# Modulation's PSUM bank, the y loads and the final projection put in another order, with the opening's modulation first

## The chip, the cores and the metric

The kernel runs on one core of one Trainium2 chip. The metric is the device time of one execution in microseconds (us), taken as the median of several runs. TensorE (PE) multiplies, with its weight loads shown apart (PEld); VectorE (DVE), ScalarE (ACT) and GpSimd (POOL) do elementwise work; SyncE (SP) issues every transfer here, on one queue.

## The reference

Two layers over 256 context tokens and 1024 latent tokens with 1024 features, then a last norm of the latent tokens. Every layer has the same frame:

```python
def rmsnorm(x, w):
    xf = x.astype(F32)
    y = xf * lax.rsqrt(jnp.mean(xf * xf, axis=-1, keepdims=True) + RMS_EPS)
    return (y * w.astype(F32)).astype(x.dtype)

def modulate(h, shift, scale):
    return h * (1 + scale) + shift
```

Shift, scale and gate of a layer come from one small product: SiLU of the conditioning vector (another one for context tokens) times a 1024 x 3072 matrix, plus a bias. Layer 0 projects the modulated input to two branches. Branch A is a bidirectional linear recurrence (RG-LRU) behind a short convolution, with sigmoid gates; branch B is attention in a band of 128 tokens to each side plus the context. Each is multiplied by its own SiLU gate, and the concatenation goes through one output projection. Layer 1 is a bidirectional gated linear recurrence in chunks (HGRN2) with eight heads, again with an output projection. Each projection is multiplied by the gate and added to the stream.

## The kernel before

Everything is held feature-major: 128 features on the partitions, tokens along the free dimension. The tokens form three chunks: c=0 and c=1 are 512 latent tokens each, c=2 is the 256 context tokens. A float32 product is made from three matmuls over split values (high and low part of the weight, high and low part of the data: `mm3`, `steps3`, line 104). `load_w` fetches a weight (line 90), ScalarE makes w_hi (line 94), GpSimd, or with `split` GpSimd and VectorE by halves, makes w_lo (line 95).

TensorE's order is that of the code in three stretches (`order_0` for the opening, `order_pe` for attention, `order_c` for layer 1 and the end). Each other engine has one fixed order too, which the scheduler chose from dependences and priorities when the program was built; `tc.high_priority` moves an instruction ahead of others that could stand there. Tiles come from pools with a number of buffers for each tag; who asks for a buffer waits until its last reader is done.

The places of this case:
- **Opening.** `load_x(c)` fetches xin of a chunk. `rms0(c)` squares its eight feature blocks on ScalarE, adds them in pairs on VectorE (line 283), sums over the partitions by matmuls n_ps with a column of ones (line 287), and spreads the reciprocal root n_r over the partitions by transposes n_pr (line 229) and a copy to n_rs (line 231). `ada_mm(l, g)` multiplies four loaded `ada` tiles by the conditioning vectors (ps_m, line 164; 32 matmuls) and copies the result to adar; `ada_fin` transposes it (ps_c, line 175), adds the bias to get mods (line 177) and, for scales, amul. `first(g, c)` applies norm and modulation to feature blocks 2g and 2g+1 of a chunk (`norm_mod`: xin, u_hi, u_lo, lines 249 to 251), then runs the first two weights' matmuls on them.
- **The loop over j = 0..7** of branch A: projection to X (line 399 copies it), convolution, gates (12 blocks of matmuls into three PSUM banks "gate"; line 437 and its neighbour apply sigmoids), two scans, products into sga. At the end of each turn one `ada_mm` runs, and its `ada_fin` runs in the next turn after X's matmuls. ps_m and ps_c share one PSUM bank, "ada".
- **out_B.** The attention output, in DRAM as yb_d, is fetched as yr and split into y_hi and y_lo (`load_yB`), and projected in a loop over eight output blocks m. acc (what branch A left, hA_d in DRAM) is loaded by line 775; VectorE adds to it (line 781).
- **The end.** `out_early` projects seven of the eight heads for chunk 0 while the last head is worked on. Then a loop over m adds the eighth head for chunk 0 (`out_m(0, full, ...)`) and makes the first half of chunk 1; a second loop makes the second half of chunk 1. Line 1051 evacuates PSUM into h; `sumsq` squares it (ScalarE, line 193) and adds into n_ss (VectorE, line 194). `final_norm` makes n_rs from n_ss (lines 212 to 231) and multiplies all eight blocks by it (line 1111).

Of the kernel before, what the change touches and what calls it, by code (L numbers as in the profile page):

```python
# [50 lines left out]
def backbone_kernel(ctx: ExitStack, tc: tile.TileContext, a: dict, out):  # L51
# [82 lines left out]
    def drain(*gens):  # L134
        for g in gens:
            for _ in g:
                pass
# [32 lines left out]
    def ada_mod(wpool, psp, l, g, bufs=NADA):  # L170
        ada_fin(psp, ada_mm(wpool, psp, l, g, bufs), l, g)

    def ada_fin(psp, row, l, g):
        pc = psp.tile([128, 512], F32, tag="ada", name="ps_c", bufs=1)
        PE.transpose(pc[:, :128], row, ident)
        with tc.high_priority(offset=PRI_E):
            V.tensor_tensor(out=mods[:, l, g], in0=pc[:, :128].rearrange("p (b x) -> p b x", x=32)[:, :, 0:2],
                            in1=adab[:, l, g].unsqueeze(2).to_broadcast([128, 4, 2]), op=ALU.add)
            if g < 4:
                V.scalar_tensor_tensor(out=amul[:, l, 2 * g:2 * g + 2], in0=mods[:, l, g, 2:4], scalar=1.0,  # L180
                                       in1=normw[:, l * 8 + 2 * g:l * 8 + 2 * g + 2].unsqueeze(2)
                                       .to_broadcast([128, 2, 2]), op0=ALU.add, op1=ALU.mult)
# [34 lines left out]
    def mean_rs(np_, ps, n):  # L217

        nb = n // 128
        r1 = np_.tile([128, 4], F32, tag="n_r1", name="n_r1", bufs=2)  # L220
        S.activation(r1[:, :nb], ps[:, :nb], AF.Sqrt, bias=eps_c)  # L221
        V.reciprocal(r1[:, :nb], r1[:, :nb])  # L222
        return r1

    def spread_rs(np_, psp, r1, n, tag, bufs, rtag="n_rs"):
        nb = n // 128
        pr = psp.tile([128, 4, 128], F32, tag=tag, name="n_pr", bufs=bufs)
        for b in range(nb):
            PE.transpose(pr[:, b], r1[:, b:b + 1].to_broadcast([128, 128]), ident)  # L229
        rs = np_.tile([128, n], F32, tag=rtag, name="n_rs", bufs=1, padded_shape=[128, 512])  # L230
        S.copy(rs, pr[:, :nb].rearrange("p a b -> p (a b)"))  # L231
        return rs

    def new_u(up, c):
        return tuple(up.tile([128, 8, CHUNKS[c][1]], F32R, tag=f"u_{p}{c}", name=f"u_{p}{c}") for p in ("hi", "lo"))
# [38 lines left out]
    def rms0(c):  # L274

        n = CHUNKS[c][1]
        ps = psA.tile([128, 512], F32, tag="gate", name="n_ps", bufs=3)
        sums = []
        for k in range(0, 8, 2):
            sq = [p0.tile([128, n], F32, tag="n_sq", name="n_sq", bufs=SQB, padded_shape=[128, 512]) for _ in range(2)]  # L280
            for i in range(2):
                S.activation(sq[i], xin[c][:, k + i], AF.Square)
            V.tensor_tensor(out=sq[0], in0=sq[0], in1=sq[1], op=ALU.add)
            sums.append(sq[0])
        for b in range(n // 128):
            for i in range(4):
                PE.matmul(ps[:, b:b + 1], sums[i][:, b * 128:b * 128 + 128], ones_m[:, 0:1], start=(i == 0),
                          stop=(i == 3))
        rs0[c] = spread_rs(p0, psA, mean_rs(p0, ps, n), n, "gate", 3, f"n_rs{c}")

    rs0 = {}

# [10 lines left out]
    def gemm_steps(w, c, psp, tag, bufs):  # L303
# [2 lines left out]
        yield from steps3(ps[:, :n], gemm_terms(w, c), n)  # L306
        return ps[:, :n]

    u = [new_u(up, c) for c in range(3)]
    apool, apool_st = open_pool("apool", side="right")  # L310

    order_0 = tc.manual_schedule(engines={PE.engine})
    order_0.__enter__()
    load_x(2)
    load_x(0)
    rms0(2)
    rms0(0)
    ada_mod(apool, psA, 0, 0, 8)
    w_first = [load_w(a["w0"][i], split=True) for i in (0, 8)]
    ps_first = {}  # L320

    def first(g, c):
# [6 lines left out]
        for i in range(2):  # L329
            mm3(ps_first[i, c], [(w_first[i][0][:, k * 128:k * 128 + 128], w_first[i][1][:, k * 128:k * 128 + 128],  # L330
                                  u[c][0][:, k], u[c][1][:, k]) for k in (2 * g, 2 * g + 1)], g == 0, g == 3)

    first(0, 2)
    row = ada_mm(apool, psA, 0, 1, 8)
    load_x(1)
    first(0, 0)
    ada_fin(psA, row, 0, 1)
    first(1, 2)
    first(1, 0)
    rms0(1)  # L340
# [62 lines left out]
    for j in range(8):  # L403
# [20 lines left out]
        if j < 7:  # L424
            X_next = x_proj(j + 1)
        if j:
            ada_fin(psA, row, *ada_lg)
        R, I, A, M = ([rg.tile([128, W], F32, tag=t_, name=t_, bufs=2) for _ in range(2)] for t_ in "RIAM")

        for d in range(2):  # L430
# [338 lines left out]
    hp0, hp0_st = open_pool("hp0")  # L769
    acc, n1ss = {}, {}  # L770

    def out_B(cs, yB, npool, psp, tag, bufs):
        for c in cs:
            acc[c] = npool.tile([128, 8, CHUNKS[c][1]], F32, tag=f"acc{c}", name=f"acc{c}")
            SY.dma_start(acc[c], hA_d[c])
            n1ss[c] = npool.tile([128, CHUNKS[c][1]], F32, tag=f"n1ss{c}", name="n1ss")
        for m in range(8):
            w = load_w(a["wo0"][8 + m], split=cs == (1,))
            for c in cs:
                ps, gt = out_half(w, m, yB[c], c, psp, tag, bufs)  # L780
                V.scalar_tensor_tensor(out=acc[c][:, m], in0=ps, scalar=gt, in1=acc[c][:, m],  # L781
                                       op0=ALU.mult, op1=ALU.add)
                if c < 2:
                    SY.dma_start(h1_d[:, m, c * 512:c * 512 + 512], acc[c][:, m])
                sumsq(npool, n1ss[c], acc[c][:, m], m)

    def load_yB(c):
        yB[c] = new_y(c)
        for k in range(8):
            split_y(yrp, yb_d[k // 2][c][:, k % 2], CHUNKS[c][1], *yB[c], k)  # L790

    yB = {}
    load_yB(2)
    load_yB(0)
    load_yB(1)
    out_B((2, 0), yB, hp0, psB, "mmo", 2)
    psB_st.close()
    psC, psC_st = open_pool("psC", space=PSUM)
    hp, hp_st = open_pool("hp", side="right")
# [245 lines left out]
    def out_m(c, sl, m, ks, w, ss=None):  # L1045

        n = sl.stop - sl.start
        ps = psC.tile([128, 512], F32, tag="mm", name="mm_o", bufs=4)
        yield from steps3(ps[:, :n], [(w[0][:, i * 128:i * 128 + 128], w[1][:, i * 128:i * 128 + 128],
                                       yT[c][:, k, 0, sl], yT[c][:, k, 1, sl]) for i, k in ks], n)  # L1050
        V.scalar_tensor_tensor(out=h2[c][:, m, sl], in0=ps[:, :n], scalar=mods[:, 1, 4 + m // 4, m % 4, 0:1],  # L1051
                               in1=h2[c][:, m, sl], op0=ALU.mult, op1=ALU.add)
        if ss is not None:
            sumsq(fq, ss, h2[c][:, m, sl], m if sl.start == 0 else (m - 4) % 8)

    full = slice(0, 512)

# [66 lines left out]
    for m in range(8):  # L1124
        w = ws[m] = load_m(m) if m > 1 else last_w[1 + m]
        SY.dma_start(h2[1][:, m], h1_d[:, m, 512:1024])
        drain(out_m(0, full, m, [(m, 7)], wk, ss[0]))
        drain(out_m(1, half[0], m, [(k, k) for k in range(8)], w, ss[1]))
    norms = [final_norm(0, full, ss[0]), final_norm(1, half[0], ss[1])]
    for g in norms:  # L1130
        next(g)
    for m in (4, 5, 6, 7, 0, 1, 2, 3):
        if m in (6, 7):
            drain(norms.pop(0))

        drain(out_m(1, half[1], m, [(k, k) for k in range(8)], ws[m] if m > 3 else load_m(m), ss[2]))
# [90 lines left out]
```

## Time and profile before

| | us |
|---|---|
| median of three runs | 1970.53 (1968.96 to 1972.46) |
| the profiled execution | 1970.83 |
| its span | 1969.0 |
| TensorE busy in it | 1877.2 (95%) |
| VectorE busy | 1134.1 (58%) |
| ScalarE busy | 954.6 (48%) |
| GpSimd busy | 467.0 (24%) |

The span goes from the first to the last instruction in the trace; 1.8 us of the execution's time lie around it. Shares are of the span. The granted clock of TensorE was 0.986 on the mean; it has two levels, 1.0 (2.4 GHz) and 0.5 (1.2 GHz).

### The profile page before, as it was taken

The numbers are of one execution on the slowest core, as the hardware profiler recorded it, in microseconds if no ns is written. First come the engines' busy times: TensorE is split into PE (matmuls) and PEld (weight loads), VectorE is DVE, ScalarE is ACT, GpSimd is POOL, SyncE is SP. The second block draws the span as 40 slices with busy tenths as digits, with TensorE's granted clock in tenths as the row PEclk, the third lists the DMA queues.
The fourth block names the chain that finished last, engine by engine and source line by source line (L and its number), as shares of the span: only waits on it lengthen the run. The fifth ranks groups of instructions, "written<-read, shape, count | busy, mean of one in ns | idle before, by whom it ended". The sixth has DMA issues, their size and how long they took to land. (4 is left out here: it accounts for less than half of the span.)

```text
span 1969.0 us, 36589 instructions
## 1 busy us (share of the span) xinstructions
PE 1877.2 (95%) x15228; PEld 1599.7 (81%) x15228; DVE 1134.1 (58%) x1920; ACT 954.6 (48%) x1766; POOL 467.0 (24%) x309
## 2 busy tenths in 40 slices
PE   6989999999999999999998999999999999999896
PEld 5778888889888787788777889888887987888686
DVE  3766555554456555656534757375557447555656
ACT  4478666683146668555642442443443334334332
POOL 0133323330111114213232212121221122122342
PEclk8999999999999999999999999999999999999998
DMA  8222333322633436435435231111111101011643
GB/s 320 88 97 92 110 102 107 99 100 101 198 113 103 128 101 192 144 119 174 142 115 201 92 109 45 33 55 35 45 52 34 53 29 61 23 54 39 252 142 115
DMA packets 89462, 207.53 MB, mean 105 GB/s; under 512 B 9808, under 2 KB 38224, under 8 KB 88272
## 3 DMA queue, kind: packets, MB, share of 16 engines
q1 hardware_dynamic: 89296, 205.20, 31.6%
q8 instruction: 119, 1.95, 0.4%
q14 instruction: 47, 0.39, 0.1%
HBM read 155.36 MB, written 49.81 MB: 104 GB/s over the span
## 5 line engine op out<-in xcount | busy, mean ns | idle before, releaser
L95 POOL TENSOR_TENSOR w_lo<-w_raw,w_hi 128x1024 fp32r<-128x1024 f32 (+2 forms) x137 | 314.9, 2302 | 1109.3 <-ACT w_hi L94 1059.7
L104 PE MATMUL mm<-u_hi,w_hi 128*128 128x512 f32 (+1 forms) x1456 | 547.3, 376 | 6.7 <-DVE sga L423 3.7
L104 PE MATMUL mm<-u_lo,w_hi 128*128 128x512 f32 (+1 forms) x1456 | 527.6, 362 | 4.9 <-DVE u_lo L251 4.9
L104 PE MATMUL mm<-u_hi,w_lo 128*128 128x512 f32 (+1 forms) x1456 | 527.3, 362 | 0.0
L104 PEld LDWEIGHTS mm<-u_hi,w_hi 128*128 128x128 f32 x1456 | 276.1, 190 | 54.5 <-issue 9.3
L104 PEld LDWEIGHTS mm<-u_lo,w_hi 128*128 128x128 f32 x1456 | 276.8, 190 | 42.4 <-DVE u_lo L251 6.9
L104 PEld LDWEIGHTS mm<-u_hi,w_lo 128*128 128x128 f32 x1456 | 275.9, 189 | 43.2
L94 ACT CAST w_hi<-w_raw 128x1024 fp32r<-128x1024 f32 (+2 forms) x163 | 141.7, 884 | 195.3 <-PE mm L104 77.8
L104 PE MATMUL mmo<-y_hi,w_hi 128*128 128x512 f32 (+1 forms) x384 | 146.1, 380 | 7.4 <-DVE acc L781 7.4
L600 DVE CUSTOM_DVE_ANT_0 p<-s_ps,maskA 128x640 f32<-128x640 f32 (+2 forms) x160 | 110.4, 713 | 59.6 <-PE s_ps L595 59.5
L611 ACT ACTIVATE p<-p,nm 128x640 f32<-128x640 f32 (+2 forms) x160 | 118.7, 743 | 42.8 <-DVE nm L607 39.2
L104 PE MATMUL mmo<-y_hi,w_lo 128*128 128x512 f32 (+1 forms) x384 | 137.5, 358 | 0.0
L104 PE MATMUL mmo<-y_lo,w_hi 128*128 128x512 f32 (+1 forms) x384 | 137.0, 357 | 0.0
L628 ACT COPY pt<-t 128x512 f32<-128x512 f32 x168 | 94.7, 581 | 82.5 <-PE t L625 82.1
L104 PE MATMUL mm_v<-w_hi,u_hi 128*128 128x256 f32 x400 | 115.2, 288 | 0.0
L104 PE MATMUL mm_v<-w_lo,u_hi 128*128 128x256 f32 x400 | 113.1, 283 | 0.0
L104 PE MATMUL mm_v<-w_hi,u_lo 128*128 128x256 f32 x400 | 113.1, 283 | 0.0
L946 DVE TENSOR_TENSOR KK<-KK,tot 128x1280 f32<-128x1280 f32 x48 | 80.1, 1670 | 41.0 <-PE lv L932 23.9
L625 PE MATMUL t<-ident,p 128*128 128x128 f32 x672 | 98.5, 274 | 4.3 <-ACT pt L628 2.7
L104 PE MATMUL mm_o<-yT,w_hi 128*128 128x256 f32 (+1 forms) x384 | 92.1, 334 | 8.2 <-DMA yT<-y_d 3.1
L625 PEld LDWEIGHTS t<-ident,p 128*128 128x128 f32 x672 | 80.7, 141 | 19.1 <-ACT pt L628 4.7
L104 PEld LDWEIGHTS mmo<-y_hi,w_hi 128*128 128x128 f32 x384 | 73.4, 191 | 22.4 <-issue 8.1
(219 smaller groups left out, 3462.6 us busy)
## 6 DMA issues: line engine op xcount, KB each, us to landing
w_raw<-w_in SPq DMA_DIRECT2D x66, 512.0 KB, 3.7
ada<-ada_w_in SPq DMA_DIRECT2D x48, 512.0 KB, 6.4
w_raw<-wo_in SPq DMA_DIRECT2D x32, 512.0 KB, 3.7
qt<-q_d SPq DMA_DIRECT2D x20, 512.0 KB, 4.9
y_d<-yhl SPq DMA_DIRECT2D x14, 512.0 KB, 3.1
yT<-y_d SPq DMA_DIRECT2D x14, 512.0 KB, 11.0
w_raw<-wo1m_in SPq DMA_DIRECT2D x12, 512.0 KB, 3.8
xin<-hT_in SPq DMA_DIRECT2D x5, 1024.0 KB, 9.2
```

The source lines that it names most:

```text
L94: S.copy(hi[:, o:m], raw[:, o:m])
L95: eng.tensor_tensor(out=lo[:, o:m], in0=raw[:, o:m], in1=hi[:, o:m].bitcast(F32), op=ALU.subtract)
L104: ins = PE.matmul(ps, l, r, start=(first and i == 0), stop=(last and i == n - 1))
L600: V.tensor_tensor_reduce(out=p[:, :nk], in0=s_ps[:, c0[x]:c0[x] + nk], in1=self.msks[x], scale=1.0, scalar=NEG, op0=ALU.add, op1=ALU.max, ...
L611: S.activation(p, p, AF.Exp, scale=0.125, bias=nm[:, x:x + 1], accum_out=dn[:, x:x + 1])
L625: PE.transpose(pt[:, h], self.P[h][:, o:o + 128], ident)
L628: S.copy(ptc, pt)
L946: V.tensor_tensor(out=kv_, in0=kv_, in1=custom(tot, 1, [[2, nb // 2], [nb - 1, 2], [0, hb]]), op=ALU.mult)
```

## The change

It has four parts.
- The opening: modulation's first product stands ahead of the two large chunks. The transfers are asked for as xin of chunk 2, ada, the first two weights, xin of chunk 0, ada, xin of chunk 1. `rms0` adds the squares in fours instead of pairs, so half as many n_ps matmuls are left. `warm(n)` issues n matmuls of a constant by itself into a PSUM tile that nothing reads.
- In the loop over j, `ada_fin` copies ps_c to SBUF on ScalarE, and VectorE reads the copy.
- In out_B, the fetching and splitting of chunk 1's y goes, one block at a time, between the weights of the first loop.
- At the end, half 0 of chunk 1 goes ahead of chunk 0's last term, the final norms begin behind the second loop's first block, and evacuation and `sumsq` in `out_m` have a high priority.

```diff
-    def ada_fin(psp, row, l, g):
+    def ada_fin(psp, row, l, g, pool=None):
         pc = psp.tile([128, 512], F32, tag="ada", name="ps_c", bufs=1)
         PE.transpose(pc[:, :128], row, ident)
         with tc.high_priority(offset=PRI_E):
-            V.tensor_tensor(out=mods[:, l, g], in0=pc[:, :128].rearrange("p (b x) -> p b x", x=32)[:, :, 0:2],
+            mc = pc[:, :128].rearrange("p (b x) -> p b x", x=32)[:, :, 0:2]
+            if pool:
+                m_sb = pool.tile([128, 4, 2], F32, tag="m_sb", name="m_sb", bufs=2)
+                S.copy(m_sb, mc)
+                mc = m_sb
+            V.tensor_tensor(out=mods[:, l, g], in0=mc,
...
             V.tensor_tensor(out=sq[0], in0=sq[0], in1=sq[1], op=ALU.add)
+            if k % 4:
+                V.tensor_tensor(out=sq[0], in0=sq[0], in1=sums.pop(), op=ALU.add)
             sums.append(sq[0])
         for b in range(n // 128):
-            for i in range(4):
+            for i in range(2):
...
-        rs0[c] = spread_rs(p0, psA, mean_rs(p0, ps, n), n, "gate", 3, f"n_rs{c}")
+        r1 = mean_rs(p0, ps, n)
+        warm(4)
+        rs0[c] = spread_rs(p0, psA, r1, n, "gate", 3, f"n_rs{c}")
...
+    def warm(n):
+
+        ps = psA.tile([128, 512], F32, tag="gate", name="ps_w", bufs=3)
+        for _ in range(n):
+            PE.matmul(ps[:, :128], ones_m, ones_m, start=True, stop=True)
...
     load_x(2)
-    load_x(0)
+    warm(20)
     rms0(2)
-    rms0(0)
-    ada_mod(apool, psA, 0, 0, 8)
+    row = ada_mm(apool, psA, 0, 0, 8)
+    warm(3)
+    ada_fin(psA, row, 0, 0)
     w_first = [load_w(a["w0"][i], split=True) for i in (0, 8)]
...
+    load_x(0)
+    warm(16)
     first(0, 2)
+    rms0(0)
+    warm(8)
+    first(0, 0)
     row = ada_mm(apool, psA, 0, 1, 8)
     load_x(1)
-    first(0, 0)
+    warm(3)
     ada_fin(psA, row, 0, 1)
+    warm(8)
     first(1, 2)
     first(1, 0)
     rms0(1)
...
-            ada_fin(psA, row, *ada_lg)
+            ada_fin(psA, row, *ada_lg, rg)
...
             w = load_w(a["wo0"][8 + m], split=cs == (1,))
+            if beside:
+                next(beside)
...
             split_y(yrp, yb_d[k // 2][c][:, k % 2], CHUNKS[c][1], *yB[c], k)
+            yield
...
-    load_yB(2)
-    load_yB(0)
-    load_yB(1)
-    out_B((2, 0), yB, hp0, psB, "mmo", 2)
+    drain(load_yB(2), load_yB(0))
+    out_B((2, 0), yB, hp0, psB, "mmo", 2, load_yB(1))
...
+        drain(out_m(1, half[0], m, [(k, k) for k in range(8)], w, ss[1]))
         drain(out_m(0, full, m, [(m, 7)], wk, ss[0]))
-        drain(out_m(1, half[0], m, [(k, k) for k in range(8)], w, ss[1]))
     norms = [final_norm(0, full, ss[0]), final_norm(1, half[0], ss[1])]
-    for g in norms:
-        next(g)
-    for m in (4, 5, 6, 7, 0, 1, 2, 3):
-        if m in (6, 7):
+    for i, m in enumerate((4, 5, 6, 7, 0, 1, 2, 3)):
+        if i == 1:
+            for g in norms:
+                next(g)
+        if i in (2, 3):
             drain(norms.pop(0))
```

TensorE's order at the very start of the program, before (mm is first's product, w_hi and w_lo its weight):

```order
L287 MATMUL n_ps<-ones_m,n_sq 128x1 x8
L229 MATMUL n_pr<-ident,n_r_176 128x128 x2
L287 MATMUL n_ps<-ones_m,n_sq 128x1 x16
L229 MATMUL n_pr<-ident,n_r_221 128x128 x4
L164 MATMUL ps_m<-ada,cc 32x128 x32
L175 MATMUL ps_c<-ident,adar 128x128
L104 MATMUL mm<-u_hi_137,w_hi 128x256
```

The same place in the changed program:

```order
L322 MATMUL ps_w<-ones_m 128x128 x20
L294 MATMUL n_ps<-ones_m,n_sq 128x1 x4
L322 MATMUL ps_w<-ones_m 128x128 x4
L234 MATMUL n_pr<-ident,n_r_193 128x128 x2
L164 MATMUL ps_m<-ada,cc 32x128 x32
L322 MATMUL ps_w<-ones_m 128x128 x3
L175 MATMUL ps_c<-ident,adar 128x128
L322 MATMUL ps_w<-ones_m 128x128 x16
L104 MATMUL mm<-u_hi_137,w_hi 128x256
```

Chunk 0's norm (16 n_ps and 4 n_pr) has gone from ahead of ps_m to behind first's products of chunk 2.

SyncE's queue ahead of out_B, before (yb_d is the attention output by head group, hA_d_80 what branch A left for chunk 2, hA_d_78 for chunk 0):

```order
L90 DMA w_raw<-wo_in 128x1024
L692 DMA yr<-yb_d_70 128x512
L692 DMA yr<-yb_d_73 128x512 x2
L775 DMA acc_9922<-hA_d_80 128x2048
L692 DMA yr<-yb_d_76 128x512 x2
L775 DMA acc_9925<-hA_d_78 128x4096
```

The same stretch of the changed program:

```order
L90 DMA w_raw<-wo_in 128x1024
L797 DMA acc_9967<-hA_d_80 128x2048
L797 DMA acc_9970<-hA_d_78 128x4096
L714 DMA yr<-yb_d_70 128x512
L714 DMA yr<-yb_d_73 128x512
L90 DMA w_raw<-wo_in 128x1024
L808 DMA h_d<-acc_9970 128x512
```

Both loads of acc have moved ahead of the last five yr loads, which now stand among the loop's weights and stores.

VectorE in the second loop of the end, before (h_17743 is chunk 0, h_18387 chunk 1):

```order
L1051 SCALAR_TENSOR_TENSOR h_18387<-mm_o,mods,h_18387 128x256 x2
L194 TENSOR_TENSOR n_ss<-n_ss,n_sq 128x256
L1111 SCALAR_TENSOR_TENSOR h_17743<-h_17743,fnw,n_rs 128x512 x8
L1051 SCALAR_TENSOR_TENSOR h_18387<-mm_o,mods,h_18387 128x256 x2
L1111 SCALAR_TENSOR_TENSOR h_18387<-h_18387,fnw,n_rs 128x256
L194 TENSOR_TENSOR n_ss<-n_ss,n_sq 128x256
L1111 SCALAR_TENSOR_TENSOR h_18387<-h_18387,fnw,n_rs 128x256 x7
```

The same place in the changed program (h_17822 is chunk 0, h_18466 chunk 1):

```order
L1135 SCALAR_TENSOR_TENSOR h_17822<-h_17822,fnw,n_rs 128x512 x3
L1075 SCALAR_TENSOR_TENSOR h_18466<-mm_o,mods,h_18466 128x256
L1135 SCALAR_TENSOR_TENSOR h_17822<-h_17822,fnw,n_rs 128x512
L199 TENSOR_TENSOR n_ss<-n_ss,n_sq 128x256
L1135 SCALAR_TENSOR_TENSOR h_17822<-h_17822,fnw,n_rs 128x512 x3
L1075 SCALAR_TENSOR_TENSOR h_18466<-mm_o,mods,h_18466 128x256
L1135 SCALAR_TENSOR_TENSOR h_17822<-h_17822,fnw,n_rs 128x512
L199 TENSOR_TENSOR n_ss<-n_ss,n_sq 128x256
L1135 SCALAR_TENSOR_TENSOR h_18466<-h_18466,fnw,n_rs 128x256 x2
```

The eight products of the final norm, one block before, are now cut by evacuations and sums.

## Rows read from the trace of the kernel before

**Rows 1.** The page: span, and TensorE's busy time with its share.
```profile
span 1969.0 us, 36589 instructions
PE 1877.2 (95%) x15228; PEld 1599.7 (81%) x15228; DVE 1134.1 (58%) x1920; ACT 954.6 (48%) x1766; POOL 467.0 (24%) x309
```
**Rows 2.** Waits of TensorE over the span: total us, times, longest us.
```profile
PE n_ps L287 <- DVE n_sq L283: 11.1, 5, 8.5
PE mmo L104 <- DVE acc L781: 7.4, 2, 6.8
PE n_ps L212 <- DVE n_ss L194: 5.3, 3, 2.9
PE ps_m L164 <- DVE mods L177: 5.0, 1, 5.0
...
PE mm_o L104 <- ACT n_rs L231: 2.0, 1, 2.0
...
PE mm_o L104 <- POOL w_lo L95: 1.7, 2, 1.1
```
**Rows 3.** Windows: stretch, its length, busy us by engine, PEclk, DMA share, GB/s.
```profile
8.00:30.00 22.00, 16.85 (x119) 14.80 (x119) 5.15 (x12) 9.81 (x22) 0.00 (x0) 1.00 1.01 406
57.00:81.00 24.00, 22.73 (x208) 18.07 (x198) 22.35 (x42) 12.56 (x22) 2.58 (x1) 0.96 0.23 65
141.00:148.00 7.00, 6.29 (x38) 4.54 (x40) 0.65 (x2) 3.57 (x5) 1.08 (x1) 0.51 0.55 187
1035.00:1043.00 8.00, 3.75 (x20) 3.75 (x21) 2.53 (x4) 3.03 (x5) 4.91 (x3) 0.57 0.90 315
1892.00:1899.00 7.00, 5.82 (x25) 5.62 (x26) 2.48 (x3) 0.63 (x1) 0.58 (x1) 0.51 0.00 0
1929.00:1934.00 5.00, 4.66 (x26) 4.69 (x27) 0.36 (x2) 0.26 (x1) 0.00 (x0) 0.66 0.01 3
1933.00:1961.00 28.00, 22.94 (x190) 22.50 (x189) 20.93 (x31) 8.24 (x15) 9.97 (x4) 0.99 0.38 132
```
**Rows 4.** Timeline of the opening: start us, busy us, engine, idle before.
```profile
7.28 1.95 ACT L282 ACTIVATE n_sq<-xin 128x256 f32<-128x256 f32 x6 [3.61 <-DMA xin<-hT_in]
...
24.53 1.12 PE L229 MATMUL n_pr<-ident,n_r 128*128 128x128 f32 x4 [0.57 <-DVE n_r L222]
...
37.65 2.39 PE L164 MATMUL ps_m<-ada,cc 128*32 128x128 f32 x64
...
51.18 3.63 PE L287 MATMUL n_ps<-ones_m,n_sq 128*128 128x1 f32 x32
...
56.27 0.58 ACT L231 COPY n_rs<-n_pr 128x512 f32<-128x512 f32 x1 [1.17 <-PE n_pr L229]
56.89 1.41 DVE L249 SCALAR_TENSOR_TENSOR xin<-xin,amul,n_rs 128x512 f32<-128x512 f32 x2 [1.57 <-ACT n_rs L231]
```
**Rows 5.** Timeline of turn j=1 at the gates.
```profile
135.63 0.58 ACT L399 COPY X<-mm 128x512 f32<-128x512 f32 x1
...
141.71 0.63 PE L164 MATMUL ps_m<-ada,cc 128*32 128x128 f32 x2 [5.04 <-DVE mods L177]
```
**Rows 6.** Timelines of SyncE's queue, VectorE and TensorE at out_B's start.
```profile
1030.81 0.42 SPq L775 DMA_DIRECT2D acc<-hA_d  x1
...
1038.71 0.48 DVE L781 SCALAR_TENSOR_TENSOR acc<-mmo,mods,acc 128x256 f32<-128x256 f32 x1 [1.23 <-DMA acc<-hA_d]
...
1039.25 0.58 PE L104 MATMUL mmo<-y_hi,w_hi 128*128 128x256 f32 x1 [6.83 <-DVE acc L781]
```
**Rows 7.** Timelines of TensorE and VectorE in the end's two loops.
```profile
1893.18 0.79 PE L104 MATMUL mm_o<-yT,w_hi 128*128 128x512 f32 x1 [1.97 <-DVE yT L1036]
...
1938.61 2.41 DVE L194 TENSOR_TENSOR n_ss<-n_ss,n_sq 128x256 f32<-128x256 f32 x1 [0.84 <-ACT n_sq L193]
1940.94 9.73 DVE L1111 SCALAR_TENSOR_TENSOR h<-h,fnw,n_rs 128x512 f32<-128x512 f32 x8
...
1959.49 0.42 DVE L194 TENSOR_TENSOR n_ss<-n_ss,n_sq 128x256 f32<-128x256 f32 x1 [0.54 <-ACT n_sq L193]
```

More of the change, by code (lines that the diff above doesn't have):

```diff
@@ L283, in rms0 @@
             V.tensor_tensor(out=sq[0], in0=sq[0], in1=sq[1], op=ALU.add)
+            if k % 4:
+                V.tensor_tensor(out=sq[0], in0=sq[0], in1=sums.pop(), op=ALU.add)
             sums.append(sq[0])
         for b in range(n // 128):
-            for i in range(4):
+            for i in range(2):
                 PE.matmul(ps[:, b:b + 1], sums[i][:, b * 128:b * 128 + 128], ones_m[:, 0:1], start=(i == 0),
-                          stop=(i == 3))
-        rs0[c] = spread_rs(p0, psA, mean_rs(p0, ps, n), n, "gate", 3, f"n_rs{c}")
+                          stop=(i == 1))
+        r1 = mean_rs(p0, ps, n)
+        warm(4)
+        rs0[c] = spread_rs(p0, psA, r1, n, "gate", 3, f"n_rs{c}")
     rs0 = {}
@@ L770, in backbone_kernel, with out_B @@
     acc, n1ss = {}, {}
-    def out_B(cs, yB, npool, psp, tag, bufs):
+    def out_B(cs, yB, npool, psp, tag, bufs, beside=None):
         for c in cs:
@@ L1050, in out_m @@
                                        yT[c][:, k, 0, sl], yT[c][:, k, 1, sl]) for i, k in ks], n)
[L1051 to L1054, printed above, removed]
+        with tc.high_priority(offset=PRI_E):
+            V.scalar_tensor_tensor(out=h2[c][:, m, sl], in0=ps[:, :n], scalar=mods[:, 1, 4 + m // 4, m % 4, 0:1],
+                                   in1=h2[c][:, m, sl], op0=ALU.mult, op1=ALU.add)
+            if ss is not None:
+                sumsq(fq, ss, h2[c][:, m, sl], m if sl.start == 0 else (m - 4) % 8)
     full = slice(0, 512)
```

## The prediction

> **What bounds the kernel now.** The first view is the page's count of busy time: TensorE works 1877.2 of 1969.0 us [rows 1], so what the change can win is what TensorE idles, about 90 us, and what it loses at the lower clock. The second is the table of TensorE's waits: squares of the first norms 11.1 us, acc 7.4, sums of the last norms 5.3, mods 5.0, n_rs 2.0, w_lo 1.7 [rows 2]. These six stand in the four places that the change touches; they sum to 32.5 us. The third is the table of windows: right behind a long wait the granted clock is 0.51 to 0.66 [rows 3], which is mostly the lower of the two levels (1.2 for 2.4 GHz), so a wait costs more than its length: a matmul in such a stretch takes about twice as long. The last view is the timeline around each wait, to see who is late and what is late next.
>
> The profiled execution took 1970.83 us, 1.8 more than its span and 0.3 more than the median; the sum is made against it.
>
> **Part A, the opening.** Before, xin2 is there at 7.28, when ScalarE begins its squares [rows 4], and everything up to 30 us moves at 406 GB/s [rows 3], so the order of the queue decides what can start. Behind xin2 now stand four ada tiles and two weights (3.1 MB) and then xin0 (2.1 MB): 5.2 MB at 406 GB/s is 12.9 us, so xin0 is complete at 20.1. TensorE does modulation and chunk 2 meanwhile. Squares of xin0, at 0.6 us each (twice the 0.33 of a 256-column one, [rows 4]) and with ScalarE also busy with chunk 2's u_hi, end between 23 and 25.3. Behind them, step by step: the sums in fours 1.4; 8 matmuls n_ps 1.8 (32 records took 3.63 [rows 4], each matmul makes two); 4 constant products and 4 transposes 1.9 (x4 took 1.12 [rows 4]); the copy 0.6 [rows 4]; two products, u_hi and u_lo 2.2 (0.70 for a product [rows 4]); 12 matmuls 2.8. first(0,0) thus ends at about 34.6. The rest up to chunk 1's norm (ps_m, ps_c, mods, first(1,2), first(1,0)) lay before between ps_m's start at 37.65 and n_ps's at 51.18 [rows 4], 13.5 with first(0,0)'s 2.8 among them, so 10.7 now: to 45.3. From there to the copy of n_rs were 5.1 (51.18 to 56.27, [rows 4]); half the n_ps records save 1.8, 4 constant products add 0.8: 4.1. n_rs of chunk 1 would be copied at 49.4 if the clock holds, against 56.27; where one or two of the waits lower the clock again, each costs 1 to 1.5, so I take 51.0. From there on, VectorE and TensorE have the same work in the same order: VectorE is busy 22.35 of 24 us between 57 and 81 [rows 3], so what is won ahead of it shifts it as a whole. **Gain 5.3 us** (3 to 7.5). The 70 constant products are nothing on the sum where they stand in waits: at 0.15 to 0.28 each (1.12 for four [rows 4]) they are 10 to 20 us, and the waits that they stand in are the 11.1 for squares [rows 2] and those for mods and u_hi behind them. Without that cover, the 16 ahead of first(0,2) could last up to 2 us longer than the wait for u, which is in the lower bound. Four extra adds on VectorE (0.7 each) stand in the sums' 1.4.
>
> **Part B, the bank.** In turn j=1 TensorE reached the next ps_m at 136.67 and waited 5.04 us for mods [rows 5], which stands on VectorE behind scans and products; both use the one bank "ada". Behind the wait the clock is 0.51 over 6.29 us of work [rows 3]; at full clock these would take 3.2, so 3.1 are lost at most, and I take 2.8, since matmuls this short do not halve in full. Now ScalarE copies ps_c right behind X's last copy, which ends at 136.21 [rows 5]; an 128x8 copy I put at 0.2 (nothing so small is in the rows; the 128x512 one is 0.58 [rows 5], the upper bound), so the bank is free at about 136.4, before TensorE asks. **Gain 5.04 + 2.8 - 0.2 = 7.6** (5 to 8.3). The other six turns show no such wait (the table has one, [rows 2]), so they win nothing. What they pay is one copy on ScalarE, ahead of the gates' sigmoids; with three banks for gates, 0.2 per turn hides behind the matmuls of the next gate. mods itself stays late on VectorE, and nothing reads it until layer 1 or out_A.
>
> **Part C, acc.** The load of acc2 was issued at 1030.81 behind three yr loads, landed at 1038.6, and VectorE's first product ran at 1038.71; TensorE, with two banks for mmo full, waited 6.83 [rows 6], at 0.57 of the clock in 1035 to 1043 [rows 3]. Now acc2 follows w_raw, some 3 us earlier, and nothing but w_raw is ahead of it: 1.6 MB from 1027.9 at the 315 GB/s of that window [rows 3] land near 1033. TensorE ran dry at 1039.25 - 6.83 = 1032.4, so a wait of about 1.7 stays (product 0.48 included [rows 6]); a second of 0.6 too. 7.4 - 2.3 is 5.1; the 3.75 us of work at 0.57 [rows 3] lose 1.6 to the clock, which the shorter wait may or may not bring down: I count 0.4 of it. **Gain 5.5** (3 to 7). The yr loads now lie between weights in the m loop; they are wanted first by the second half, 60 us later, which covers them.
>
> **Part D, the end.** In the m loop, half 1's seven early terms now cover the wait for yT's low part (1.97 [rows 7]), but the first half of m=2 then asks for w_lo sooner: one was late by 1.1 already [rows 2], and ScalarE's cast ahead of it still stands behind squares of m=1. With the clock at 0.51 there [rows 3] as before, I give the m loop 0.9. The second loop has eight out_m of 24 matmuls at 0.12 (22.94 us for 190 records, [rows 3]), 23.0, and 2.5 of norms' matmuls: 25.5 without gaps. Before, 5.6 came on top: 2.4 of the waits for n_ss (5.3 less the longest, 2.9 [rows 2]), 2.0 for n_rs [rows 2], 1.2 at 0.66 of the clock [rows 3]. The norms' matmuls now have an out_m behind which n_ss gets ready, and evacuations pass the final products. So TensorE could be done 0.9 + 5.6 = 6.5 earlier.
> VectorE cannot follow all of it. While GpSimd makes w_lo, its instructions with two inputs from SBUF stand: one sum took 2.41 us instead of 0.42, and eight products 9.73 instead of 8 x 0.70 [rows 4, 7]. Four w_lo lie in 1933 to 1961 (9.97 us of GpSimd, [rows 3]). After the change the sixteen products begin two out_m and a norm into the loop, which starts near 1925 (0.9 earlier than before): 5.8 and 1.8 behind it, near 1932.5 instead of 1940.94 [rows 7], under three w_lo: 7 us of stalls, 8.8 of products, 4.5 of evacuations and sums among them bring VectorE to 1952.8, and the last three evacuations with sums (3.0) to 1955.8, against 1959.91 [rows 7]. **Gain 4.1** (0.5 to 8).
> The Trainium skill's page "SBUF — State Buffer", section "SBUF: two separate sides", says that a VectorE instruction with two SBUF inputs and a GpSimd instruction that reads SBUF lock each other out for the whole instruction; the 2.41 agrees. By that rule part D is worth 4.1; if the port did not count it would be 6.5.
>
> **Sum.** 5.3 + 7.6 + 5.5 + 4.1 = 22.5, so 1970.8 - 22.5 = 1948.3; I say 1948.
>
> **The rivals.**
> Opening and end give half or nothing: A's waits only move (u_lo on VectorE is late instead of n_ps, at the lower clock), and D's m loop waits for w_lo. For it: VectorE is saturated right behind the opening [rows 3], and the 1.1 for w_lo [rows 2]. Half of A (2.6) and D at 0 leave 15.7: 1955.
> All four waits go and the clock never falls: A 7.5, B 8.3, C 7, D 8, in all 30.8: 1940. For it: the falls that the rows show stand behind waits of 1.97, 5.04 and 6.83 us [rows 5 to 7], and shorter ones would be left. Against it: by the sums above, C's 1.7 and two waits of the opening stay near the first of these.
> The bank is free but TensorE then waits for the gates' banks, which ScalarE empties: B gives 3, not 7.6, 1953. Against it: X's copy and the first sigmoids follow without idle time at 136.1 [rows 5].
> Slower: ScalarE's copy delays the gates in each of seven turns. It decides only from 22.5 / 7 = 3.2 us per turn on; the bound on one copy is 0.58 [rows 5], 4 us in seven turns: 1952. To end at 1975 it would need 3.9 a turn.
> The change does nothing: the bank, the queue and the order differ in the rows above, so I give this only what is in "same".
>
> **How the numbers follow.** Forecast 1948 (its own range 1943 to 1952.5): 0.60. Half of opening and end, 1955: 0.20. All gone, 1940: 0.12. Gates' banks, 1953: 0.04. Slower, 1975 or more: 0.02; no change: 0.02. 0.2% is 3.9 us, about what a measurement of this kernel tells from no change. Leaving out 0.06 at each end (half of the 1940 case, the outer part of the 1955 one) gives 1940 to 1957. Faster 0.94, same 0.03, slower 0.03.
>
> **What would show it.** A: n_rs of chunk 1 copied at 49 to 52, and the first gates 5 us earlier. B: no wait of ps_m for mods, full clock behind it. C: acc2 issued right behind w_raw, one wait under 2.5 us. D: no wait inside the second loop; the last n_ss 4 us behind TensorE's last out_m. Wrong would be: a chunk 0 norm after 28 us, a wait at the gates for ScalarE in all turns, or products that take 2.4 us each.

## The result, and the profile after

The changed kernel takes 1951.77 us (median of 4 runs, 1949.79 to 1954.98) where the kernel before takes 1971.44 on the same chip: a ratio of 0.9904, 95% interval 0.989 to 0.9917, or 18.9 us less. The prediction was 1948.

The page of the changed kernel, its span and its line of busy times:

```profile
span 1950.1 us, 36796 instructions
PE 1878.0 (96%) x15328; PEld 1604.3 (82%) x15328; DVE 1141.2 (59%) x1926; ACT 955.1 (49%) x1773; POOL 468.8 (24%) x309
```

TensorE is as busy as before [rows 1], although the opening has half the sums n_ps and 70 constant products more. By the records of these two groups (busy 15.2 us for n_ps before; 6.6 for n_ps and 22.5 for the constant products now) the rest of its work took some 13 us less: time at half clock went, besides some 20 us of idle time. TensorE's waits in the changed kernel (total, times, longest):

```profile
...
PE n_ps L294 <- DVE n_sq L290: 6.1, 4, 1.8
PE n_ps L217 <- DVE n_ss L199: 5.6, 1, 5.6
...
PE mm_o L104 <- POOL w_lo L95: 2.5, 2, 1.9
PE mmo L104 <- DVE acc L805: 2.4, 2, 1.8
...
PE gate L104 <- ACT I L459: 1.6, 1, 1.6
...
PE mm_o L104 <- DVE yT L1059: 1.5, 1, 1.5
...
PE mm_o L104 <- ACT w_hi L94: 1.3, 1, 1.3
```

Against [rows 2]: mods is gone from the table, acc is down from 7.4 to 2.4, squares from 11.1 to 6.1. New are a wait of the gates for ScalarE's sigmoid and one for the third weight's w_hi; the waits for w_lo grew from 1.7 to 2.5. The sums n_ss have one wait instead of three, but it is 5.6 us long and stands at the very end.

Windows at the places of [rows 3] (columns as there, PEclk behind the five busy times):

```profile
20.00:30.00 10.00, 6.45 (x37) 5.95 (x37) 5.25 (x10) 4.94 (x10) 0.00 (x0) 0.77 1.02 417
30.00:40.00 10.00, 10.00 (x95) 9.21 (x98) 5.00 (x8) 4.58 (x8) 0.00 (x0) 0.72 0.51 202
135.00:146.00 11.00, 9.42 (x108) 7.86 (x107) 2.68 (x4) 9.61 (x13) 6.47 (x3) 1.00 0.64 207
1020.00:1035.00 15.00, 12.59 (x77) 10.89 (x76) 4.49 (x7) 6.34 (x11) 5.23 (x3) 1.00 0.88 342
1888.00:1898.00 10.00, 10.00 (x67) 9.66 (x68) 4.56 (x8) 3.60 (x6) 7.44 (x4) 0.83 0.77 238
```

In the loop (135 to 146) and in out_B (1020 to 1035) the clock now stays full. In the opening it is low between 24 and 36, and in the end's first loop it still falls.

How the 18.9 us came about is read from marks that both traces have. Start of the first scan of branch A: 125.96 before, 121.95 after. Fifth scan (turn j=1): 169.81, 159.33. First scan of the last turn: 454.30, 442.92. A late product of VectorE in out_B's second half: 1132.79, 1115.08. Last add into n_ss: 1959.91, 1940.79. One pair of executions can mislead here, as the last section shows, so the table takes the mean length of a stage over all profiled kernels that have the same code in it:

| part, stage | without the part (kernels) | with it (kernels) | gain | forecast |
|---|---|---|---|---|
| A: start to first scan | 126.4 (4) | 121.7 (6) | 4.7 | 5.3 |
| B: first scan to first attention product | 436.6 (4) | 429.8 (9) | 6.9 | 7.6 |
| C: late attention to layer 1's first norm | 195.9 (4) | 190.8 (10) | 5.1 | 5.5 |
| D: from there to the last add into n_ss | 805.9 (4) | 802.4 (5) | 3.5 | 4.1 |

The first attention product is VectorE's first one with the mask (line 600 before), late attention its 145th of 160; layer 1's first norm is taken at the copy of chunk 1's n_rs. In every stage the kernels with the part lie apart from those without it: 120.9 to 123.4 against 126.0 to 126.7, 429.6 to 430.0 against 436.1 to 436.8, 190.2 to 191.6 against 195.5 to 196.4, 801.6 to 803.5 against 805.2 to 806.5.

The gains sum to 20.2, within the interval of the timed 18.9 (16.4 to 21.7).

### The profile page after: what moved, and what is told of

Same layout as the page of the kernel before. It is cut to its first block, busy times and chain, and to the rows that moved or that the text cites. A ratio compares the mean times of both kernels' runs of the same rounds, so it can differ in the third digit from the quotient of the medians.

```text
span 1950.1 us, 36796 instructions
## 1 busy us (share of the span) xinstructions
PE 1878.0 (96%) x15328; PEld 1604.3 (82%) x15328; DVE 1141.2 (59%) x1926; ACT 955.1 (49%) x1773; POOL 468.8 (24%) x309
## 3 DMA queue, kind: packets, MB, share of 16 engines
q8 instruction: 120, 1.97, 0.4%
## 4 chain that ended last, share of the span: by engine, by line
PE 78%; DVE 13%; ACT 4%; issue 3%; DMA 2%; POOL 1%; SPq 0%; DVEq 0%; ACTq 0%; POOLq 0%
PE mm L104 35%; PE mmo L104 10%; PE mm_v L104 7%; PE pv L661 4%; PE t L647 3%; PE mm_o L104 3%; PE gate L104 3%; PE s_ps L616 2%; PE pv L1000 2%; PE s_ps L617 2%; PE lv L943 1%; DVE uc L432 1%; PE po L1030 1%; PE pk L992 1%; DVE h L1135 1%
## 5 line engine op out<-in xcount | busy, mean ns | idle before, releaser
L639 POOL COPY rd<-dn 128x128 f32<-128x128 f32 x80 | 24.8, 310 | 272.2 <-DVE dn L636 115.1
```

## The experiments

Each was timed against the kernel before on the same chip; gains in us are 1 minus the ratio, of 1971.

### One part alone: a_only, b_only, c_only, d_only

Each is the kernel before with the changed lines of one part of the diff shown above, for instance for B these (cut to its main lines):

```diff
+            if pool:
+                m_sb = pool.tile([128, 4, 2], F32, tag="m_sb", name="m_sb", bufs=2)
+                S.copy(m_sb, mc)
+                mc = m_sb
...
-            ada_fin(psA, row, *ada_lg)
+            ada_fin(psA, row, *ada_lg, rg)
```

> The kernel before with part A alone (opening re-ordered, squares in fours, constant products). Read from the two traces, chunk 1's n_rs comes 3.7 us earlier and the first scan 4.0 us earlier. If the parts add up, this gives 4.0 us (1967.4 for 1971.4). If the opening's gain is partly given back in turn j=1, where TensorE waits for mods anyway (mods stands on VectorE, which shifts as a whole), the same 4.0; if that wait is set by something that does not shift, less than 2.

> The kernel before with part B alone (ScalarE copies ps_c, the bank is free for the next ps_m). Read from the traces: 6.5 us at turn j=1 and 0.2 us in each later turn, of which 0.4 is lost again behind the loop: 7.0 us (1964.4) if the parts add up. The prediction said 7.6. The rival (the gates' banks take over) would be about 3.

> The kernel before with part C alone (acc loads ahead of chunk 1's y loads). Read from the traces 6.5 us (1964.9): 5.0 us of waits and 1.5 us of the clock. The prediction said 5.5, with the clock mostly lost either way; then 5.0.

> The kernel before with part D alone (order and priorities of the end). Read from the traces 1.4 us (1970.0), within what a measurement tells from nothing; the prediction said 4.1 (1967.3).

| kernel | ratio | 95% interval | gain, us |
|---|---|---|---|
| a_only | 0.9971 | 0.9958 to 0.9983 | 5.7 |
| b_only | 0.9978 | 0.9965 to 0.9991 | 4.3 |
| c_only | 0.998 | 0.997 to 0.999 | 3.9 |
| d_only | 0.9988 | 0.9978 to 0.9998 | 2.4 |

All four are faster, but two expectations were missed: b_only gained 4.3 (1.8 to 6.9) where 7.0 was said, c_only 3.9 (2.0 to 5.9) where 6.5 was. In the trace of b_only the loop is the expected 7.0 us shorter (321.34 for 328.34 from the first scan to the first of the last turn); attention behind it, with the same code, took 2.7 more (last section). The 6.5 for C was read from one pair of traces; the table has 5.1. D's 2.4 (0.4 to 4.3) agrees with the 1.4 of the one pair of traces as well as with the 4.1 of the prediction. The gains sum to 16.3, uncertain by some 4.5, against 18.9: within the noise the parts add up, and an interplay of a few us would not show.

The wait at the bank went, but not without a successor. ScalarE at turn j=1 of the changed kernel, and TensorE behind it:

```profile
131.61 0.58 ACT L421 COPY X<-mm 128x512 f32<-128x512 f32 x1
132.08 0.17 ACT L180 COPY m_sb<-ps_c 128x8 f32<-128x8 f32 x1
...
136.23 1.36 ACT L460 ACTIVATE M<-R,sneg 128x1284 f32<-128x1284 f32 x1 [1.62 <-DVE M L483]
```

```profile
138.22 0.50 PE L104 MATMUL gate<-uh,w_hi 128*128 128x512 f32 x1 [1.58 <-ACT I L459]
```

The copy takes 0.17 and comes right behind X's. TensorE then waits 1.58 for a sigmoid: ScalarE's Tanh into M waits for VectorE to let go of M (L483, the sums behind the scans), and the sigmoids behind it in ScalarE's order stand too. So VectorE's scans still hold TensorE, by another way, for 1.58 instead of 5.04 [rows 5]; and as the clock does not fall behind that wait, most of the gain stays.

### The constant products: no_warm

```diff
-    warm(20)
...
-        warm(4)
...
-    warm(16)
...
-    warm(8)
```
(and so on: all 70 out)

> The changed kernel without any of the constant products. If they hold the clock up, the opening's chains run at half clock more often and this is 2 to 4 us slower than the changed kernel (1954 to 1956 for 1951.8). If they mostly stand in the way (in the changed kernel's trace 4 of them delay chunk 0's transposes by 1.2 us and 8 of them first(0,0) by 0.9 us, at half clock), this is the same or up to 2 us faster (1950 to 1952).

Ratio 0.9899 (0.9882 to 0.9916): the same as the changed kernel's 0.9904; the first scan starts at 121.97, against 121.95. Its windows:

```profile
20.00:30.00 10.00, 6.47 (x27) 6.00 (x27) 5.25 (x10) 4.93 (x10) 0.00 (x0) 0.50 1.02 414
30.00:40.00 10.00, 7.61 (x36) 5.16 (x40) 5.03 (x8) 4.05 (x7) 0.00 (x0) 0.51 0.50 198
```

Both effects are in the traces, and cancel. Without constant products TensorE is at half clock from 20 to 40 us; with them it is at 0.77 and 0.72, but they stand in the way. TensorE in the changed kernel:

```profile
24.34 0.38 PE L294 MATMUL n_ps<-ones_m,n_sq 128*128 128x1 f32 x2 [1.81 <-DVE n_sq L290]
26.43 3.15 PE L294 MATMUL n_ps<-ones_m,n_sq 128*128 128x1 f32 x14 [1.70 <-DVE n_sq L290]
29.44 2.05 PE L322 MATMUL ps_w<-ones_m 128*128 128x128 f32 x8
31.28 1.06 PE L234 MATMUL n_pr<-ident,n_r 128*128 128x128 f32 x4
32.14 3.62 PE L322 MATMUL ps_w<-ones_m 128*128 128x128 f32 x16
35.41 0.58 PE L104 MATMUL mm<-u_hi,w_hi 128*128 128x512 f32 x1
```

Behind two waits of 1.81 and 1.70 that hold no constant products, the sums run at half clock: 3.15 us for 14 records, where 32 took 3.63 at full [rows 4]. The constant products that follow are at half clock as well and last twice as long as meant; the 8 ahead of first(0,0) end at 35.76, when u_hi had been there since 34.5.

### The constant products where the waits are: warm_fill

```diff
-    warm(16)
+    warm(12)
     first(0, 2)
+    warm(8)
     rms0(0)
-    warm(8)
+    warm(4)
     first(0, 0)
...
+                if c == 0 and b == i == 0:
+                    warm(7)
         r1 = mean_rs(p0, ps, n)
-        warm(4)
+        warm(2)
```

> The changed kernel with the constant products moved: 8 and 7 of them into the two waits of 1.8 and 1.7 us ahead of and inside chunk 0's sums (where the clock falls), 12 for 16 ahead of first(0,2), 4 for 8 ahead of first(0,0), 2 for 4 inside each norm. If the fall of the clock comes from those two waits, n_ps and what follows run at full clock and chunk 1's n_rs comes 2 to 4 us earlier: 1948 to 1950. If the fall has another cause, the same as the changed kernel within 1 us.

Ratio 0.9879 (0.986 to 0.9897): 4.9 us less than the changed kernel, uncertain by 4.5. The first scan starts at 119.37, against a mean of 121.7 for the opening as changed: 2.3 us. From 20 to 30 the clock did what was expected (the 14 records of the sums take 1.72 instead of 3.15); from 33.5 on it still falls, behind a wait of 1.32 for u_hi:

```profile
20.00:30.00 10.00, 9.28 (x74) 8.51 (x73) 5.25 (x11) 5.52 (x11) 0.00 (x0) 1.00 1.02 415
30.00:40.00 10.00, 8.39 (x91) 6.31 (x91) 5.25 (x10) 4.84 (x10) 0.00 (x0) 0.83 0.67 242
```

### GpSimd's reads: end_memset and end_keep

```diff
-                eng.tensor_tensor(out=lo[:, o:m], in0=raw[:, o:m], in1=hi[:, o:m].bitcast(F32), op=ALU.subtract)
+                if zero:
+                    eng.memset(lo[:, o:m].bitcast(F32), 0.0)
+                else:
+                    eng.tensor_tensor(out=lo[:, o:m], in0=raw[:, o:m], in1=hi[:, o:m].bitcast(F32), op=ALU.subtract)
...
-        drain(out_m(1, half[1], m, [(k, k) for k in range(8)], ws[m] if m > 3 else load_m(m), ss[2]))
+        drain(out_m(1, half[1], m, [(k, k) for k in range(8)], ws[m] if m > 3 else load_m(m, True), ss[2]))
```

> The changed kernel, but the four w_lo of the last loop's reloaded weights (m=0 to 3) are set to zero by GpSimd instead of computed; it leaves out the low part of these four weights for the second half of chunk 1. GpSimd then writes SBUF but does not read it. If the port that GpSimd reads through is what stretches VectorE's products (4.3 us for three), they take 0.7 each, VectorE is done about 1.5 us behind TensorE's last block instead of 5.45, and the time falls by 4 us to 1948. If VectorE's products are slow for another reason, 0 to 1 us.

```diff
-        drain(out_m(1, half[1], m, [(k, k) for k in range(8)], ws[m] if m > 3 else load_m(m), ss[2]))
+        drain(out_m(1, half[1], m, [(k, k) for k in range(8)], ws[m] if m not in (2, 3) else load_m(m), ss[2]))
```

> The changed kernel, with weights 0 and 1 of the end's second loop taken from the buffers where they still lie instead of loaded and split again; GpSimd has two w_lo fewer, and the two that stay run early in the loop. If GpSimd's w_lo are what stretches VectorE's products, six products of 4.3 us for three lose most of their stalls, VectorE is done 2 to 3 us behind TensorE's last block instead of 5.45, and the time falls by 2.5 to 3.5 us, to 1948 to 1949.5. If it is the writing of SBUF or VectorE's own work, 0 to 1 us.

end_memset: 0.9866 (0.9847 to 0.9885), end_keep: 0.9875 (0.9863 to 0.9888), against 0.9904 for the changed kernel. VectorE in the changed kernel, with the GpSimd instruction that it meets:

```profile
1919.02 2.40 DVE L199 TENSOR_TENSOR n_ss<-n_ss,n_sq 128x256 f32<-128x256 f32 x1 [0.84 <-ACT n_sq L198]
1921.34 4.27 DVE L1135 SCALAR_TENSOR_TENSOR h<-h,fnw,n_rs 128x512 f32<-128x512 f32 x3
```

```profile
1918.75 2.40 POOL L95 TENSOR_TENSOR w_lo<-w_raw,w_hi 128x1024 fp32r<-128x1024 f32 x1 [1.79 <-ACT w_hi L94]
1922.02 2.39 POOL L95 TENSOR_TENSOR w_lo<-w_raw,w_hi 128x1024 fp32r<-128x1024 f32 x1 [0.87 <-ACT w_hi L94]
```

VectorE in end_memset, the same two groups, and GpSimd beside the second:

```profile
1917.82 0.42 DVE L202 TENSOR_TENSOR n_ss<-n_ss,n_sq 128x256 f32<-128x256 f32 x1 [0.85 <-ACT n_sq L201]
1918.29 2.08 DVE L1138 SCALAR_TENSOR_TENSOR h<-h,fnw,n_rs 128x512 f32<-128x512 f32 x3
```

```profile
1919.84 0.96 POOL L96 MEMSET w_lo<- 128x1024 f32 x1 [2.31 <-PE mm_o L107]
```

Three products take 2.08 with a GpSimd instruction beside their end that writes 128x1024 without reading (the next three, from 1921.68, take 2.07 with one at 1922.90), and 4.27 beside one that reads. That GpSimd is busy, or writes, does not matter here; that it reads does. The Trainium skill's page "SBUF — State Buffer" (section "Who interferes with whom") states just this: two SBUF inputs on VectorE contend with a GpSimd instruction that reads SBUF, not with one that only writes it. What it costs the end is seen in TensorE's wait for the last n_ss, first in the changed kernel, then in end_keep (1.64 in end_memset):

```profile
1940.94 0.98 PE L217 MATMUL n_ps<-ones_m,n_ss 128*128 128x1 f32 x4 [5.60 <-DVE n_ss L199]
```

```profile
1935.96 0.60 PE L217 MATMUL n_ps<-ones_m,n_ss 128*128 128x1 f32 x4 [1.55 <-DVE n_ss L199]
```

Two w_lo fewer suffice, since the two that stay (from 1913.57 and 1917.75) are done before the products begin at 1920.34. In the traces both give 4 us at that wait, as was expected of end_memset and more than the 2.5 to 3.5 of end_keep; the timed gains over the changed kernel, 7.5 and 5.7 us, are uncertain by 3 to 5.

### The third weight's cast: end_early

```diff
+    ws[0], ws[1] = last_w[1:]
+    ws[2] = load_m(2)
     for m in range(8):
-        w = ws[m] = load_m(m) if m > 1 else last_w[1 + m]
+        w = ws[m]
+        if 1 < m + 1 < 8 and m + 1 not in ws:
+            ws[m + 1] = load_m(m + 1)
```

> The changed kernel, with the third weight of the end's first loop asked for ahead of the loop, so that ScalarE's cast of it stands ahead of the squares instead of behind them (its load landed 15 us before). If the cast's place sets the waits of 1.26 and 1.94 us at m=2, both go, and most of the half clock behind them (1.7 us): 3.2 to 4.9 us at TensorE's end. VectorE follows with its products; if it is held by GpSimd's w_lo to the same extent, the time falls by the same 3 to 5 us, to 1947 to 1949. If the w_lo themselves on GpSimd are the limit, under 1 us.

Ratio 0.9902 (0.9886 to 0.9919): nothing. Both waits at m=2 went, as expected, and two others came in their place. VectorE and TensorE of end_early:

```profile
1876.73 5.22 DVE L1059 TENSOR_TENSOR yT<-on,yT 128x512 fp32r<-128x512 f32 x2
```

```profile
1882.01 0.58 PE L104 MATMUL mm_o<-yT,w_hi 128*128 128x256 f32 x1 [3.67 <-DVE yT L1059]
...
1895.00 0.39 PE L104 MATMUL mm_o<-yT,w_lo 128*128 128x256 f32 x1 [1.82 <-POOL w_lo L95]
```

The w_lo that was brought forward now runs on GpSimd while VectorE makes the low part of yT from two SBUF inputs: 5.22 us instead of 3.07 for the same two instructions in the changed kernel. TensorE waits 3.67 instead of 1.52, and the clock falls behind it (0.63 from 1882 to 1890). The other new wait, 1.82, is for the next weight's w_lo, whose cast at 1891.46 again stands behind squares. Neither theory had this: the cast's place was the cause of the waits at m=2, and GpSimd's reads and the next weight took the gain.

### The price of ScalarE's copy: bank_copy8

```diff
-                S.copy(m_sb, mc)
+                for _ in range(8):
+                    S.copy(m_sb, mc)
```

> The changed kernel with ScalarE's copy of ps_c made eight times instead of once in each of the seven turns. One copy took 0.17 us, so this puts some 1.2 us on ScalarE ahead of the gates' sigmoids in each turn. If that place is on the path (the slower rival), the loop gets 6 to 8 us longer, 1958 to 1960; if the banks for gates hide it in the turns but not in j=1, where TensorE already waits 1.6 us for a sigmoid, 1 to 2 us, 1953; if it is hidden everywhere, 0.

Ratio 0.9952 (0.9937 to 0.9967): 9.5 us slower than the changed kernel, uncertain by 4, so the 6 to 8 of the first case lie within it. But the time is not lost where that case had it. From the first scan to the first of the last turn the loop is 12.1 us longer (333.07 for 320.97): 4.3, 5.3, 0.5 and 2.7 us in the four turns from j=2 on, nothing in the others. TensorE waits for a gate's bank only 0.3 us there on account of the copies. It waits for sga, which VectorE multiplies: 12.0 us in four waits, where the changed kernel has 3.6. The first of them, with VectorE and GpSimd ahead of it:

```profile
206.18 3.41 DVE L484 TENSOR_TENSOR M<-M 128x1024 f32<-128x1024 f32 x1
...
206.00 2.51 POOL L95 TENSOR_TENSOR w_lo<-w_raw,w_hi 128x1024 fp32r<-128x1024 f32 x1 [5.67 <-ACT w_hi L94]
...
211.45 0.54 PE L104 MATMUL mm<-u_hi,w_hi 128*128 128x512 f32 x1 [3.56 <-DVE sga L446]
```

The same two instructions in the changed kernel:

```profile
207.75 1.22 DVE L483 TENSOR_TENSOR M<-M 128x1024 f32<-128x1024 f32 x1
...
208.04 4.65 POOL L95 TENSOR_TENSOR w_lo<-w_raw,w_hi 128x1024 fp32r<-128x1024 f32 x1 [6.14 <-ACT w_hi L94]
```

Here GpSimd's w_lo starts 0.18 us ahead of VectorE's sum and the sum takes 3.41; there it starts 0.29 behind it, the sum takes 1.22 and w_lo 4.65. The same holds at 262 and 372 (3.40 and 3.41, waits of 3.53), and not at 320, where the sum takes 1.22 and the wait is 1.37. So most of what the eight copies cost is again VectorE beside GpSimd's reads: 7.9 of the 12.1 us are what these three waits grew by, and the clock falls behind them (0.97 from 200 to 260, 0.95 from 260 to 330). It is no price of ScalarE's time at the gates, and why the copies make the two instructions change places is not shown. Of the one copy of 0.17 the run says little; in the changed kernel the turns behind j=1 got 0.1 to 0.2 us shorter, the last 0.03 longer.

### Together: best and best_no_warm

best has warm_fill's constant products, end_keep's weights, and end_early's cast with w_lo of that one weight on VectorE, behind yT (of its diff only this line; `load_m` and `load_w` hand the engine on):

```diff
+    ws[2] = load_m(2, V)
```

> The changed kernel with three mends: the constant products moved as in warm_fill (2.0 us at the first scan there), weights 0 and 1 kept as in end_keep (2.5 to 3.5), and the third weight's cast early with its w_lo on VectorE, behind yT's low part, so that GpSimd's reads do not meet that part (in end_early they did, and the wait for yT grew from 1.53 to 3.67). The last takes the waits of 1.26 and 1.94 at m=2 and the clock's fall behind them: 3 to 5 us. Sum 7.5 to 10.5: 1941.5 to 1944.5.

best: 1936.31 us, ratio 0.9824 (0.9811 to 0.9836), 34.7 us less than before and 15.8 less than the changed kernel. VectorE in the end's first loop:

```profile
1868.77 3.08 DVE L1062 TENSOR_TENSOR yT<-on,yT 128x512 fp32r<-128x512 f32 x2
1873.15 1.14 DVE L1078 SCALAR_TENSOR_TENSOR h<-mm_o,mods,h 128x512 f32<-128x512 f32 x2 [1.29 <-PE mm_o L104]
1874.21 1.22 DVE L95 TENSOR_TENSOR w_lo<-w_raw,w_hi 128x1024 fp32r<-128x1024 f32 x1
```

yT's low part takes 3.08 again, w_lo 1.22 behind it, and both waits at m=2 are gone. TensorE's last block ends 1.5 us ahead of the last n_ss. From the second of the two yT instructions to there it takes 53.2 us (1871.18 to 1924.41) instead of 62.1 in the changed kernel (1878.65 to 1940.79), 8.9 less. The opening gives 4.3 (first scan at 117.70 instead of 121.95). The time is 5 us below the 1941.5 to 1944.5 that were expected. Of the 17.1 us between the two spans these two places hold 13.2; another 2.7 lie in attention, whose code is the same, so part of it is the scatter of the last section.

> The kernel of best without any constant product. If they are worth what the clock gives once they stand in the waits (in best, chunk 1's n_rs is copied at 48.4; in no_warm, at 0.50 of the clock from 20 to 40 us, at 52.7), this is 3 to 4.5 us slower than best: 1939.5 to 1941. If most of what warm_fill won came from fewer of them in the way, it is within 1 us of best.

best_no_warm: 1942.02 us, ratio 0.9849 (0.9817 to 0.988). By the ratios it is 4.9 us slower than best, uncertain by 7, so the time alone does not decide. The first scan says more: it starts at 121.97 and 122.62 in the two traces without constant products (no_warm, best_no_warm), at 119.37 and 117.70 in the two with them in the waits (warm_fill, best), at 120.9 to 123.4 in the six with them as in the change. Placed in the waits, constant products are worth some 4 us of the opening (3.8 on the mean); placed as in the change, they were worth nothing that can be measured.

## Why the prediction was right

The time lies in the stated range and in the likeliest case's own (1943 to 1952.5), at its slow end, and by the table of stages each part gave what its row said, a little less each time.

**A** was 5.3 and measured 4.7. The order of the queue worked as worked out: xin0's squares on ScalarE ended at 24.9, inside the 23 to 25.3. The step that was mis-sized is chunk 0's norm: n_ps was taken at full clock (1.8 for all) and the constant products as fillers of waits. The last 14 records of the sums took 3.15 us at half clock, and the constant products some 2 us of the path (n_pr starts at 31.28, 1.2 us behind the reciprocal that it needs, and first(0,0) 0.9 behind u_hi). first(0,0) ended at 38.5 instead of 34.6; what follows was quicker than said, and chunk 1's n_rs came at 52.54, where 51.0 was forecast. One of the prediction's own signs of being wrong, a chunk 0 norm after 28 us, did appear: the sums end at 29.6 and n_rs is copied at 32.38. That the total holds all the same is in part luck: the 1.6 us set aside for the clock, without a place, took up some of it. A row of the kernel before could have warned, for the same sums ran at half clock there too, 26 records in 5.71 where 32 took 3.63 [rows 4]:

```profile
18.26 5.71 PE L287 MATMUL n_ps<-ones_m,n_sq 128*128 128x1 f32 x26 [0.45 <-DVE n_sq L283]
```

That the gain passes on as a whole was right: 3.7 at n_rs, 4.0 at the first scan.

**B** was 7.6 and measured 6.9. The bank came free at 132.25, TensorE has no wait there, and the clock stayed up. Not foreseen as part of the likeliest case, but as a rival, was the gates' wait for ScalarE: 1.58 of the 5.04 came back. What balanced it in part, by luck, are some 0.9 us over the later turns, in which the forecast had said they win nothing. At turn j=1 itself 6.5 of the forecast 7.6 were won.

**C** was 5.5 and measured 5.1. TensorE's first wait at acc, its row in the changed kernel against the 6.83 of [rows 6]:

```profile
1023.01 0.39 PE L104 MATMUL mmo<-y_hi,w_hi 128*128 128x256 f32 x1 [1.83 <-DVE acc L805]
```

1.7 was said for it and 0.6 for the second; they are 1.83 and 0.58. The clock did not fall behind them, so more than the 0.4 came back there: at the last sum into n1ss, on the mean of the kernels of the table, 5.6 are won, and 0.5 is lost again up to the copy of n_rs.

**D** was 4.1 and measured 3.5, by other terms than said. TensorE's second loop has no wait inside it, as forecast, and the last n_ss comes 5.45 us behind TensorE's last block, where 4 was said: the reading of GpSimd's port was right, and end_memset and end_keep show its cause. Wrong is the term for the first loop, 0.9 won. The third weight holds it more than before: TensorE asks for its first product 1.26 before ScalarE's cast and then 1.94 before w_lo, 3.2 us instead of 1.10, and the clock falls behind it (0.83 from 1888 to 1898). Together with 1.52 for yT the first loop's waits are 4.7 us instead of 4.1. The cast could have run 7 us earlier, when ScalarE fell idle (it did in end_early); it stood behind squares in ScalarE's order.

The rival that halves A and takes D away would have given 1955; it is refuted by a_only and d_only: 2.6 lies below a_only's interval (3.3 to 8.3), 0 below d_only's (0.4 to 4.3), if only just. That the clock never falls is refuted by the windows above. That ScalarE's copy delays the gates in each turn is refuted by the turns, which got no longer (the last by 0.03). The chances of the cases with a gain add up to 0.96, where the last line of the prediction says 0.94; nothing hangs on it.

## What to carry to other kernels

In this kernel filler matmuls paid only in the waits behind which the clock fell: find these waits in the trace, put in as many as the wait is long, and take them from places where what they precede is already there. Before a stall on the longest path is moved, look which two instructions will then run side by side: a GpSimd instruction that reads SBUF made VectorE's work with two SBUF inputs 1.7 to 5.7 times as long here (3.07 to 5.22, 2.08 to 4.27, 1.22 to 3.41, 0.42 to 2.40), so work brought forward can cost what it wins. Look too which of the two starts first: a few tenths of a us decided which one stood. A buffer that frees one engine earlier shows what held the next one; the gain is the difference of the two waits, plus what half clock had cost if the clock no longer falls behind the second.

## What was not expected of the hardware

The same code takes different times. From the first attention product to the 145th, with no change between the kernels, before takes 395.2 us, b_only 397.9 and c_only 393.9; the 14 traces lie between 392.0 and 397.9. What b_only has more goes with a fall of the clock: TensorE in b_only at the start of an attention unit (granted clock 0.76 from 790 to 803), and the same place in the kernel before (1.00 from 797 to 810):

```profile
797.47 0.58 PE L599 MATMUL s_ps<-khh,qt 128*128 128x256 f32 x1 [2.56 <-DVE mx L605]
797.85 0.41 PE L600 MATMUL s_ps<-kll,qt 128*128 128x256 f32 x1
```

```profile
804.25 0.39 PE L594 MATMUL s_ps<-khh,qt 128*128 128x256 f32 x1 [2.09 <-DVE mx L600]
804.47 0.28 PE L595 MATMUL s_ps<-kll,qt 128*128 128x256 f32 x1
```

Behind 2.56 us a 256-column matmul takes 0.41, behind 2.09 it takes 0.28. The length of a wait alone does not tell, for the clock fell behind waits of 1.70 and 1.81 in the opening and of 1.97 at 1893 in the kernel before [rows 7], and not behind 1.83 at out_B in the changed one. So a stage far from a change can give or take 2 us in one execution, and a change of 3 us has to be read from several traces.

The granted clock is not reliable at the start of a trace: in best_no_warm the window from 20 to 30 us reads 1.00, while its 256-column matmuls take 0.41 to 0.42, as at half clock; in best they take 0.28. The 1.00 of [rows 3] from 8 to 30 us is to be read with the same care, for it covers the 26 sums in 5.71 us shown above.

```profile
20.00:30.00 10.00, 6.25 (x27) 5.87 (x27) 5.82 (x10) 4.67 (x9) 0.00 (x0) 1.00 1.02 413
```

```profile
21.71 0.41 PE L104 MATMUL mm<-u_hi,w_lo 128*128 128x256 f32 x1
21.92 0.42 PE L104 MATMUL mm<-u_hi,w_hi 128*128 128x256 f32 x1
```
